# A 90-degree rotation: ScalarE lines each quarter up before VectorE turns it

## The chip, the core and the metric

The kernel runs on one core of one Trainium2 chip. Its time is the device time of one execution in microseconds (us); the figure of a kernel is the median of several runs. Four parts of the core do anything here: SyncE (SP) issues every DMA, the 16 DMA engines move the data, VectorE (DVE) transposes, and ScalarE (ACT) copies. TensorE and GpSimd have no part in the work.

## The reference

```python
batch, c, h, w = 32, 3, 256, 256
x = np.random.randn(batch, c, h, w).astype(np.float32)

def reference(x):
    return np.rot90(x, k=-1, axes=(-2, -1)).astype(np.float32)
```

Each of the 96 images of 256 x 256 fp32 values is turned by 90 degrees clockwise: row h of the input, read from left to right, becomes column 255 - h of the output, read from top to bottom. No arithmetic is done. 25.17 MB are read and 25.17 MB written.

## The kernel before

All images are seen as 24576 rows of 256 values. A slab is 2048 rows (128 partitions times R = 16 rows), and the 12 slabs are taken as six pairs of 4 MB. Each pair has a tile of its own in SBUF, `u0` to `u5`, of 128 partitions x 2 slabs x 4096 values, so no tile is used twice: a pair is loaded into its tile, turned in place, and stored from there.

**Loads.** SP issues twelve loads of 2 MB at the start, one after the other, pair by pair. Pairs 1 to 5 (L59) come in with 16 rows of an image on each partition, in runs of 16 KB; even and odd partitions hold different images. Pair 0 is special (L55): its two slabs come in with two pieces of 8 rows each, second slab first, so that VectorE has a whole slab to begin on when the first 2 MB are there.

**Turning a pair.** VectorE's transpose turns blocks of 32 partitions x 32 values. In `turn_pair` the 32 values of a block are 16 column groups `g`, 16 values (64 bytes) apart, times the two slabs `a`, 4096 values (16 KB) apart; the slab runs fastest. So neighbours in the stream that is read are never neighbours in memory, and the stream that is written (`dst`) hops in the same way, 16 KB and then 64 bytes. A pair is cut in four quarters: the low and high half of the column within a group (`c`), by the low and high half of the row within a partition (`r`). Each quarter is one instruction of 2048 values on each partition. The result of a quarter lands where another quarter's source was:

- (low, low) would land on the source of (high, low), (low, high) on that of (low, low), (high, high) on that of (low, high), and (high, low) on that of (high, high).

The kernel breaks this ring with a spare tile in PSUM: (low, low) is turned into `spare[n % 2]` first (L78), the other three are turned in place, in the order of the ring (L82), and when the last of them is done ScalarE copies the held quarter home in two halves (L84), writing runs of 8 values. There are two spare tiles of 2048 values on each partition, so the next pair's turning does not wait for these copies.

Pair 0 is turned slab by slab (`turn_slab`, L65): one slab into the two spare tiles, the other into the place of the first, and then ScalarE copies the spare tiles into the second slab (L70, two copies of 2048 values).

**Stores.** SP issues two stores of 2 MB for each pair (L97), in the order of the pairs, behind all loads on the same queue. A store waits until its pair is turned and the copies are home.

What sets the order: each engine takes its instructions as they are written in the program; between engines they wait for one another where they touch the same data. SP waits in order, too: a store that is not ready holds back those behind it.

Of the kernel before, what the change touches and what calls it, by code (L numbers as in the profile page):

```python
# [1 line left out]

# [4 lines left out]


@with_exitstack  # L10
def kernel(
    ctx: ExitStack,
    tc: tile.TileContext,
    x: bass.AP,
    out: bass.AP,
):

    nc = tc.nc
    fp32 = mybir.dt.float32

    B, C, H, W = x.shape
    P = nc.NUM_PARTITIONS
    R = 16
    I = 2  # L30
    E = R * W
    n_slabs = B * C * H // (P * R)
    hw = R // 2

    rows_in = x.rearrange("b c h w -> (b c h) w")
    rows_out = out.rearrange("b c h w -> (b c h) w")

    def short(rows):
        return rows.rearrange("(n i p r) w -> n p i (r w)", i=I, p=P, r=R // I)

    def long(rows):
        return rows.rearrange("(n a i m r) w -> n i m a (r w)", a=2, i=I, m=P // I, r=R)

    ld_short, ld_long, st_long = short(rows_in), long(rows_in), long(rows_out)

    pairs = [
        ctx.enter_context(tc.tile_pool(name=f"pair{n}", bufs=1)).tile([P, 2, E], fp32, name=f"u{n}")
        for n in range(n_slabs // 2)
    ]
    psum = ctx.enter_context(tc.tile_pool(name="psum", bufs=1, space=bass.MemoryType.PSUM))  # L50
    spare = [psum.tile([P, E // 2], fp32, name=f"spare{h}") for h in range(2)]


    for s, home in ((1, 0), (0, 1)):
        nc.sync.dma_start(  # L55
            out=pairs[0][:, home].rearrange("p (i f) -> p i f", i=I), in_=ld_short[s])
    for n in range(1, len(pairs)):
        for i in range(I):
            nc.sync.dma_start(out=pairs[n][i::I], in_=ld_long[n, i])  # L59

    def turn_slab(src, dsts):
        s = src.rearrange("p (i r g c) -> p c r g i", i=I, r=R // I, c=R)
        for h, d in enumerate(dsts):
            d = d.rearrange("p (c k r) -> p c r k", c=hw, r=R // I)[:, :, ::-1, ::-1]
            nc.vector.transpose(out=d, in_=s[:, h * hw : (h + 1) * hw])  # L65

    turn_slab(pairs[0][:, 0], spare)
    turn_slab(pairs[0][:, 1], [pairs[0][:, 0, : E // 2], pairs[0][:, 0, E // 2 :]])
    for h in range(2):
        nc.scalar.copy(out=pairs[0][:, 1, h * E // 2 : (h + 1) * E // 2], in_=spare[h])  # L70

    def turn_pair(n):
        u = pairs[n]
        src = u.rearrange("p a (r g c) -> p c r g a", r=R, c=R)
        dst = u.rearrange("p i (c k r) -> p c r k i", c=R, r=R)[:, :, ::-1, ::-1, :]
        held = spare[n % 2]
        low, high = slice(0, hw), slice(hw, R)
        nc.vector.transpose(  # L78
            out=held.rearrange("p (i c k r) -> p c r k i", i=I, c=hw, r=hw)[:, :, ::-1, ::-1, :],
            in_=src[:, low, low])  # L80
        for c, r in ((low, high), (high, high), (high, low)):
            nc.vector.transpose(out=dst[:, c, r], in_=src[:, c, r])  # L82
        for i in range(I):
            nc.scalar.copy(  # L84
                out=u[:, i, : E // 2].rearrange("p (c r) -> p c r", r=R)[:, :, hw:],
                in_=held[:, i * E // 4 : (i + 1) * E // 4].rearrange("p (c r) -> p c r", r=hw))

    for n in range(1, len(pairs)):
        turn_pair(n)
    for n in range(len(pairs)):  # L90
        for a in range(2):
            if n == 0:

                st = rows_out[: 2 * P * R].rearrange("(s i m r) w -> i m s (r w)", s=2, i=I, r=R)[a]
            else:
                st = rows_out.rearrange("(n a i m r) w -> n a m i (r w)", a=2, i=I, m=P // I, r=R)[n, a]
            nc.sync.dma_start(out=st, in_=pairs[n][a::2])  # L97


# [1 line left out]
_INS = ['x']  # L101
_OUTS = [((32, 3, 256, 256), 'float32')]


# [23 lines left out]
```

## Time and profile before

| | |
|---|---|
| Time, median of 3 runs | 123.2 us (122.94 to 123.29) |
| The profiled execution | 122.98 us, of which the profile's span is 121.2 us |
| Busy in the span | VectorE 86.6 us (71%), ScalarE 14.5 us (12%) |
| DMA queue of SP | 50.33 MB, mean 415 GB/s over the span; packets fill 97.9% of 16 engines' span |
| DMA issues | 12 loads and 12 stores of 2048 KB each |

The profile shows one execution. A line such as `L82 DVE STREAM_TRANSPOSE u<-u ... x15 | 54.3, 3619` is a group of instructions: line 82 of the kernel, engine, operation, written and read tile, how many of them, their busy time in us in total, and the mean of one in ns. `SPq` is SP's queue, that is, its waits and DMA issues. "To landing" is the time from a DMA's issue to its last byte. Times in the timeline count from the start of the span.

### The profile page before, as it was taken

The numbers are of one execution on the slowest core, as the hardware profiler recorded it, in microseconds if no ns is written. First come the engines' busy times: TensorE is split into PE (matmuls) and PEld (weight loads), VectorE is DVE, ScalarE is ACT, GpSimd is POOL, SyncE is SP. The second block draws the span as 40 slices with busy tenths as digits, with TensorE's granted clock in tenths as the row PEclk, the third lists the DMA queues.
The fourth block names the chain that finished last, engine by engine and source line by source line (L and its number), as shares of the span: only waits on it lengthen the run. The fifth ranks groups of instructions, "written<-read, shape, count | busy, mean of one in ns | idle before, by whom it ended". The sixth has DMA issues, their size and how long they took to land.

```text
span 121.2 us, 125 instructions
## 1 busy us (share of the span) xinstructions
DVE 86.6 (71%) x24; ACT 14.5 (12%) x13; POOL 0.2 (0%) x4
## 2 busy tenths in 40 slices
DVE  0029999619999999999999999999999970000000
ACT  0000400380000330005000060000600023000000
POOL 0000000000000000000000000000000000000000
DMA  4999999999999999999999999999999999999994
GB/s 87 403 419 433 465 433 433 427 427 433 433 411 422 416 427 433 433 433 433 422 433 433 433 433 433 433 433 433 433 433 433 433 427 427 433 433 433 433 433 184
DMA packets 3713, 50.33 MB, mean 415 GB/s; under 512 B 385, under 2 KB 385, under 8 KB 385
## 3 DMA queue, kind: packets, MB, share of 16 engines
q1 hardware_dynamic: 3712, 50.33, 97.9%
q14 instruction: 1, 0.00, 0.0%
HBM read 25.17 MB, written 25.17 MB: 415 GB/s over the span
## 4 chain that ended last, share of the span: by engine, by line
DVE 60%; issue 13%; DMA 6%; ACT 2%; ACTq 1%
DVE u L82 33%; DVE spare L78 15%; DVE u L65 6%; DMA u<-in_x_dram 6%; DVE spare L65 6%; ACT u L70 2%; ACT u L84 1%; ACTq L123 1%
## 5 line engine op out<-in xcount | busy, mean ns | idle before, releaser
L82 DVE STREAM_TRANSPOSE u<-u 128x2048 f32<-128x2048 f32 x15 | 54.3, 3619 | 0.5
L78 DVE STREAM_TRANSPOSE spare<-u 128x2048 f32<-128x2048 f32 x5 | 17.9, 3574 | 3.7 <-ACT u L70 3.7
L84 ACT COPY u<-spare 128x1024 f32<-128x1024 f32 x10 | 9.6, 1014 | 64.6 <-DVE u L82 64.6
L65 DVE STREAM_TRANSPOSE spare<-u 128x2048 f32<-128x2048 f32 x2 | 7.1, 3585 | 8.3 <-DMA u<-in_x_dram 8.3
L65 DVE STREAM_TRANSPOSE u<-u 128x2048 f32<-128x2048 f32 x2 | 7.8, 3986 | 0.0
L70 ACT COPY u<-spare 128x2048 f32<-128x2048 f32 x2 | 3.6, 1869 | 8.7 <-DVE u L65 8.7
L70 ACT ACT_TABLE_LOAD x1 | 1.3, 1283 | 13.3 <-DMA u<-in_x_dram 13.3
L112 POOL MEMSET const-bfloat16-1.0<- 128x1 bf16 x1 | 0.1, 101 | 0.0
L112 POOL MEMSET const-uint8-127<- 128x1 uint8 x1 | 0.1, 101 | 0.0
L112 POOL MEMSET const-float32-0.0<- 128x1 f32 x1 | 0.1, 98 | 0.2 <-issue 0.2
L112 POOL MEMSET const-float32-1.0<- 128x1 f32 x1 | 0.1, 98 | 0.0
## 6 DMA issues: line engine op xcount, KB each, us to landing
u<-in_x_dram SPq DMA_DIRECT2D x12, 2048.0 KB, 31.1
out_dram<-u SPq DMA_DIRECT2D x12, 2048.0 KB, 28.3
```

The lines of the kernel that those rows point to most:

```text
L65: nc.vector.transpose(out=d, in_=s[:, h * hw : (h + 1) * hw])
L70: nc.scalar.copy(out=pairs[0][:, 1, h * E // 2 : (h + 1) * E // 2], in_=spare[h])
L78: nc.vector.transpose(out=held.rearrange("p (i c k r) -> p c r k i", i=I, c=hw, r=hw)[:, :, ::-1, ::-1, :], in_=src[:, low, low])
L82: nc.vector.transpose(out=dst[:, c, r], in_=src[:, c, r])
L84: nc.scalar.copy(out=u[:, i, : E // 2].rearrange("p (c r) -> p c r", r=R)[:, :, hw:], in_=held[:, i * E // 4 : (i + 1) * E // 4].rearrange ...
L112: nc = _bacc.Bacc("TRN2", target_bir_lowering=False, num_devices=1)
L123: with _tile.TileContext(nc) as tc:
```

## The change

For pairs 1 to 5, VectorE no longer reads the pair's tile. ScalarE copies each quarter (`take`) out of the tile in the order in which VectorE will want it, hopping through memory as VectorE did before, and writes it as one run of 2048 values into a temporary tile (`line_up`). VectorE (`turn`) reads that run and writes the turned quarter straight home, to the same places with the same hops as before. The quarters 0 to 3 are (low, low), (low, high), (high, high), (high, low); quarter 0 goes to `spare[0]`, 1 and 3 to `spare[1]`, and 2 to a new SBUF tile `extra` of 2048 values. The order in the program is take 0, take 1, take 2, turn 1, take 3, turn 2, turn 3, turn 0. The two copies home at the end of each pair are gone.

The load of the first 2 MB is cut in two transfers of 1 MB; both fill the slab that VectorE turns first. Pair 0 is turned as before. The other loads and all stores move the same bytes between the same places in the same order; their code is written anew (`pairs` becomes `groups`, all of size 2).

```diff
+    low, high = slice(0, hw), slice(hw, R)
...
+    sizes = (2,) * 6
+    first = [sum(sizes[:n]) for n in range(len(sizes))]
...
     spare = [psum.tile([P, E // 2], fp32, name=f"spare{h}") for h in range(2)]
+    extra = ctx.enter_context(tc.tile_pool(name="extra", bufs=1)).tile([P, E // 2], fp32, name="extra")
...
-    for s, home in ((1, 0), (0, 1)):
-        nc.sync.dma_start(
-            out=pairs[0][:, home].rearrange("p (i f) -> p i f", i=I), in_=ld_short[s])
-    for n in range(1, len(pairs)):
+    ld = rows_of(rows_in, 0).rearrange("(s i p r) w -> s i p (r w)", s=2, i=2, p=P)
+    home = [groups[0][:, s].rearrange("p (i f) -> p i f", i=2) for s in range(2)]
+    for i in range(2):
+        nc.sync.dma_start(out=home[0][:, i], in_=ld[1, i])
+    nc.sync.dma_start(out=home[1], in_=ld[0].transpose([1, 0, 2]))
+    for n in range(1, len(sizes)):
...
-    def turn_pair(n):
-        u = pairs[n]
+    def turn_group(n):
+        u = groups[n]
         src = u.rearrange("p a (r g c) -> p c r g a", r=R, c=R)
         dst = u.rearrange("p i (c k r) -> p c r k i", c=R, r=R)[:, :, ::-1, ::-1, :]
-        held = spare[n % 2]
-        low, high = slice(0, hw), slice(hw, R)
-        nc.vector.transpose(
-            out=held.rearrange("p (i c k r) -> p c r k i", i=I, c=hw, r=hw)[:, :, ::-1, ::-1, :],
-            in_=src[:, low, low])
-        for c, r in ((low, high), (high, high), (high, low)):
-            nc.vector.transpose(out=dst[:, c, r], in_=src[:, c, r])
-        for i in range(I):
-            nc.scalar.copy(
-                out=u[:, i, : E // 2].rearrange("p (c r) -> p c r", r=R)[:, :, hw:],
-                in_=held[:, i * E // 4 : (i + 1) * E // 4].rearrange("p (c r) -> p c r", r=hw))
+        quarters = ((low, low), (low, high), (high, high), (high, low))
+        temps = (spare[0], spare[1], extra, spare[1])
 
+        def line_up(q):
+            return temps[q].rearrange("p (c r g a) -> p c r g a", c=hw, r=hw, g=R)
+
+        def take(q):
+            c, r = quarters[q]
+            nc.scalar.copy(out=line_up(q), in_=src[:, c, r])
+
+        def turn(q):
+            c, r = quarters[q]
+            nc.vector.transpose(out=dst[:, c, r], in_=line_up(q))
+
+        take(0)
+        take(1)
+        take(2)
+        turn(1)
+        take(3)
+        turn(2)
+        turn(3)
+        turn(0)
```

More of the change, by code (lines that the diff above doesn't have):

```diff
@@ L29 @@
     R = 16
-    I = 2
     E = R * W
-    n_slabs = B * C * H // (P * R)
     hw = R // 2
+    low, high = slice(0, hw), slice(hw, R)
     rows_in = x.rearrange("b c h w -> (b c h) w")
     rows_out = out.rearrange("b c h w -> (b c h) w")
[L38 to L48, printed above, removed]
+    sizes = (2,) * 6
+    first = [sum(sizes[:n]) for n in range(len(sizes))]
+    groups = [
+        ctx.enter_context(tc.tile_pool(name=f"group{n}", bufs=1)).tile([P, s, E], fp32, name=f"u{n}")
+        for n, s in enumerate(sizes)
     ]
@@ L51, with rows_of @@
     spare = [psum.tile([P, E // 2], fp32, name=f"spare{h}") for h in range(2)]
-    for s, home in ((1, 0), (0, 1)):
-        nc.sync.dma_start(
-            out=pairs[0][:, home].rearrange("p (i f) -> p i f", i=I), in_=ld_short[s])
-    for n in range(1, len(pairs)):
+    extra = ctx.enter_context(tc.tile_pool(name="extra", bufs=1)).tile([P, E // 2], fp32, name="extra")
+    def rows_of(rows, n):
+        return rows[first[n] * P * R : (first[n] + sizes[n]) * P * R]
+    ld = rows_of(rows_in, 0).rearrange("(s i p r) w -> s i p (r w)", s=2, i=2, p=P)
@@ L58 @@
+    home = [groups[0][:, s].rearrange("p (i f) -> p i f", i=2) for s in range(2)]
[3 more added lines that the diff above has]
+    for n in range(1, len(sizes)):
+        I = sizes[n]
+        ld = rows_of(rows_in, n).rearrange("(a i m r) w -> i m a (r w)", a=2, i=I, m=P // I)
         for i in range(I):
-            nc.sync.dma_start(out=pairs[n][i::I], in_=ld_long[n, i])
+            nc.sync.dma_start(
+                out=groups[n].rearrange("p s f -> p (s f)").rearrange("p (a f) -> p a f", a=2)[i::I],
+                in_=ld[i])
@@ L61, in turn_slab @@
     def turn_slab(src, dsts):
-        s = src.rearrange("p (i r g c) -> p c r g i", i=I, r=R // I, c=R)
+        s = src.rearrange("p (i r g c) -> p c r g i", i=2, r=R // 2, c=R)
         for h, d in enumerate(dsts):
-            d = d.rearrange("p (c k r) -> p c r k", c=hw, r=R // I)[:, :, ::-1, ::-1]
+            d = d.rearrange("p (c k r) -> p c r k", c=hw, r=R // 2)[:, :, ::-1, ::-1]
             nc.vector.transpose(out=d, in_=s[:, h * hw : (h + 1) * hw])
-    turn_slab(pairs[0][:, 0], spare)
@@ L68 @@
-    turn_slab(pairs[0][:, 1], [pairs[0][:, 0, : E // 2], pairs[0][:, 0, E // 2 :]])
+    u = groups[0]
+    turn_slab(u[:, 0], spare)
+    turn_slab(u[:, 1], [u[:, 0, : E // 2], u[:, 0, E // 2 :]])
     for h in range(2):
-        nc.scalar.copy(out=pairs[0][:, 1, h * E // 2 : (h + 1) * E // 2], in_=spare[h])
-    def turn_pair(n):
-        u = pairs[n]
+        nc.scalar.copy(out=u[:, 1, h * E // 2 : (h + 1) * E // 2], in_=spare[h])
+    def turn_group(n):
+        u = groups[n]
         src = u.rearrange("p a (r g c) -> p c r g a", r=R, c=R)
@@ L88 @@
[L88 to L97, printed above, removed]
+        quarters = ((low, low), (low, high), (high, high), (high, low))
@@ new lines, in turn_group @@
+        turn(3)
+        turn(0)
+    for n in range(1, len(sizes)):
+        turn_group(n)
+    st = rows_of(rows_out, 0).rearrange("(s i m r) w -> i m s (r w)", s=2, i=2, m=P // 2)
+    for a in range(2):
+        nc.sync.dma_start(out=st[a], in_=groups[0][a::2])
+    for n in range(1, len(sizes)):
+        st = rows_of(rows_out, n).rearrange("(a i m r) w -> a m i (r w)", a=2, i=sizes[n], m=P // 2)
+        for i in range(0, sizes[n], 2):
+            for a in range(2):
+                nc.sync.dma_start(out=st[a][:, i : i + 2], in_=groups[n][a::2, i : i + 2])
```

## The prediction

> **What bounds the kernel now.** I read the page's slices and queues first, since 50.33 MB through one core suggest the transfers.
>
> ```profile
> DVE  0029999619999999999999999999999970000000
> ACT  0000400380000330005000060000600023000000
> ...
> DMA  4999999999999999999999999999999999999994
> ...
> q1 hardware_dynamic: 3712, 50.33, 97.9%
> ```
>
> The DMA engines are full from the first slice to the last; VectorE ends a fifth of the span earlier. The windows give the rate of a full stretch:
>
> ```profile
> 55.80:70.20 14.40, 14.30 (x5) 1.93 (x2) 0.00 (x0) 1.00 1.02 432
> 70.20:84.60 14.40, 14.30 (x5) 1.93 (x2) 0.00 (x0) 1.00 1.01 432
> ```
>
> VectorE is busy 14.3 of 14.4 us (one pair), ScalarE 1.93, and the queue moves 432 GB/s. A pair's 4.19 MB of stores take 4.19 / 0.432 = 9.7 us, 4.85 us for each store. So turning a pair (14.4) is slower than storing it (9.7); the transfers bound the end only because a backlog of loads and finished pairs feeds the queue. How much is left of it, the time from a store's issue to its landing says, asked window by window (pairs 2, 3, 4 and 5, two stores each, medians):
>
> ```profile
> out_dram<-u SPq DMA_DIRECT2D x2, 2048.0 KB, 30.6
> ...
> out_dram<-u SPq DMA_DIRECT2D x2, 2048.0 KB, 25.9
> ...
> out_dram<-u SPq DMA_DIRECT2D x2, 2048.0 KB, 21.2
> ...
> out_dram<-u SPq DMA_DIRECT2D x2, 2048.0 KB, 16.5
> ```
>
> The backlog falls by 4.7 us a pair, which is 14.4 - 9.7. Of the last pair, the shortest landing of all stores is 14.4, so with a median of 16.5 the other took 18.6: issued at 101.14 and about 101.8, they land at 115.5 and 120.4, and 0.8 us later the span ends. On an empty queue, 2 MB land sooner, as the first load shows in the chain (0.73 to 8.24):
>
> ```profile
> 0.73 7.51 DMA u<-in_x_dram
> ...
> 26.89 3.62 DVE spare L78
> ...
> 99.19 1.01 ACT u L84
> ```
>
> Hence the slack of the last pair is 14.4 - 7.5 = **6.9 us**: it may be ready at 101.1 + 6.9 = 108.0 instead of 101.1 before anything moves. Later than that, the span ends at ready + 7.5 + 4.85 + 0.8 = ready + 13.2. Time is span plus 122.98 - 121.2 = 1.8; the median of the runs (123.2) is 0.2 above the profiled one, and I add that too: time = ready + 15.2.
>
> The groups of instructions give the prices:
>
> ```profile
> L82 DVE STREAM_TRANSPOSE u<-u 128x2048 f32<-128x2048 f32 x15 | 54.3, 3619 | 0.5
> L78 DVE STREAM_TRANSPOSE spare<-u 128x2048 f32<-128x2048 f32 x5 | 17.9, 3574 | 3.7 <-ACT u L70 3.7
> L84 ACT COPY u<-spare 128x1024 f32<-128x1024 f32 x10 | 9.6, 1014 | 64.6 <-DVE u L82 64.6
> L65 DVE STREAM_TRANSPOSE spare<-u 128x2048 f32<-128x2048 f32 x2 | 7.1, 3585 | 8.3 <-DMA u<-in_x_dram 8.3
> L65 DVE STREAM_TRANSPOSE u<-u 128x2048 f32<-128x2048 f32 x2 | 7.8, 3986 | 0.0
> L70 ACT COPY u<-spare 128x2048 f32<-128x2048 f32 x2 | 3.6, 1869 | 8.7 <-DVE u L65 8.7
> ```
>
> All transposes move 2048 values in 3.57 to 3.99 us, whatever they write to. ScalarE's copies read and write runs: 1869 - 1014 = 855 ns for 1024 more values is 0.835 ns a value.
>
> **The change, part by part.** Call a `take` A and a `turn` D.
>
> *D.* The write stays as in L82, the read becomes a run. Which of the two made the 3.62 us no row says alone: with one and the same read, L65 costs 3585 into `spare` and 3986 into `u`, so the write side does count (0.4 us by its place). Bounds: 1.87 (the nearest row that has runs on both sides, ScalarE's L70) and 3.99 (the dearest transpose). I take 3.62, the row with the same write on the same engine: if either side's hops alone hold the stream at 3.6, curing one cures nothing.
>
> [...]
>
> *A.* Four copies of 2048 values a pair. No row has ScalarE reading with hops. Bounds: not below 1.87 (the same count in runs, L70; hops can't make it cheaper) and up to 3.57 (VectorE reading the very same pattern into the same tile, L78). I take the one between that keeps VectorE's price in engine steps: a hopping value costs VectorE 3574 / 2048 = 1.745 ns; its own step in runs is not shown, so I go by the middle of the two bounds per value (0.835 and 1.745: 1.29) and, since L78 has the same pattern and L70 only the same engine, somewhat above it: 1.4, giving A = 2048 x 1.4 + 0.16 (L84's 1.014 - 1024 x 0.835 ns) = **3.0 us**.
>
> [...]
>
> *The order.* turn 0, the last of a pair, reads `spare[0]`; the next pair's take 0 writes it, so ScalarE waits there until VectorE is done with the whole pair, with take 1 and take 2 queued behind it. VectorE's first turn needs take 1, so it stands idle for takes 0 and 1. Then turn 1 covers take 2. take 3 needs `spare[1]`, which turn 1 frees, and lies beside turn 2; turn 3 and turn 0 follow. With A up to D a pair costs 2A + 4D, with A above D it is 4A + 2D. Handovers between the engines cost 0.02 to 0.05 us each (26.87 to 26.89, 41.46 to 41.49); 0.1 a pair in all.
>
> *Sum.* 2 x 3.0 + 4 x 3.62 + 0.1 = 20.6, less the 0.1 by which two copies in a row overlap (2 x 1.87 took 3.63): **20.5 us a pair** against 14.4. Pair 1 starts at 26.9 as now, after ScalarE's L70. Ready: 26.9 + 5 x 20.5 = 129.4. Time: 129.4 + 15.2 = **144.6 us**.
>
> *Removed.* The copies home: four of five pairs' lie beside VectorE's work (windows: 1.93 of 14.4) and are worth nothing; the last pair's 1.93 us stood before its stores, and the sum has left it out already. VectorE still does four instructions a pair; nothing of its own work goes.
>
> *Loads and stores.* One more issue, 0.43 to 0.46 us of SP by the two of L55. SP's next loads move back by that; hidden, because by 8.3 us it has issued nine loads while only one has landed. Were that cover gone, 0.5 us. VectorE's first turn needs both 1 MB parts, so its start at 8.26 stands. A shorter first issue might start the flow sooner, within the 0.44 us of that issue: -0.4 to +0.5, taken as 0. `extra` and the temporaries have no queue to pass. SP's stores keep their order and now wait for turn 0.
>
> **The rivals.**
>
> *VectorE's reading was the whole cost.* D falls towards 1.87 and the chain stays under the transfers. It decides at a period of (108.0 - 26.9) / 5 = 16.2 us: with A = 1.87, D must be under 3.1; with A = 3.0, 4A + 2D must be under 16.2, so D under 2.1. Then the end is the queue's and the time 123.2, give or take the 0.4 of the first transfer. For it: L82 and L78 read alike, write to different memories, and differ by only 45 ns. Against it: L65's 0.4 us by the write alone. 22 in 100; of these 7 gain over 0.3%, 12 stay within it, 3 lose a little.
>
> *ScalarE becomes the bound.* D falls to 1.87 but A is L78's 3.57: 4 x 3.57 + 2 x 1.87 = 18.0, ready 116.9, time 132. Decides from A above 3.1 at that D. 10 in 100.
>
> *The overlap inside a pair does not come.* If a copy and a turn of one tile wait for each other although they touch different quarters, take 2 stands before turn 1 and take 3 before turn 2: 4A + 4D = 26.5, ready 159.4, time 174.6. The trace of before has no copy beside a turn of the same tile (L84 starts when the last L82 has ended), so it can't exclude this. 6 in 100.
>
> **How the numbers follow.** My forecast (D unchanged, A between its bounds) has 62 in 100. Its own range: A = 1.87 gives 18.25 a pair, ready 118.1, 133.3 us; A = 3.57 gives 21.6, ready 134.9, 150.1 us, with a little above it for D: 133 to 151. The range over the cases must go down to the hidden case: 122.8 to 151. It leaves out the lost overlap (6), gains (7) and an overshoot (about 5). About 0.3%, 0.4 us, is what can be told from no change here: faster 0.07, same 0.12, slower 0.62 + 0.10 + 0.06 + 0.03 = 0.81.
>
> **What would show it.** D: the turns' rows at 3.6 us, three of a pair reading `spare`, one `extra`. A: `take`'s mean near 3.0, bounds 1.87 and 3.57. Order: VectorE idle for two copies, about 6 us, before the first turn of each pair, released by ScalarE, and none between its four turns; ScalarE waiting on VectorE once at each pair's take 0. Transfers: the DMA row, full until about 100 us, shows gaps before the last two pairs' stores, which land in about 7.5 and 12 us instead of 14 and 19. I am wrong if D drops below 3, or the row stays full to the end.

## The result, and the profile after

The changed kernel takes 148.14 us (median of 6 runs, 148.06 to 148.20) against 123.1 us (6 runs): 1.2035 times as long, with a 95% interval of 1.2023 to 1.2047. The profiled execution took 148.19 us, with a span of 146.4 us. The forecast was 144.6 us, slower.

The page's slices and its queue line of the changed kernel:

```profile
DVE  0079993007999108999009998019997039995000
ACT  0003006999920899900999901999802999600000
...
DMA  5999999999999999999999997898000996001995
...
q1 hardware_dynamic: 3728, 50.33, 81.4%
```

The two compute engines now take turns: where one row shows a gap, the other shows nines. The DMA row is full up to about two thirds of the span and then has two empty stretches. The queue has the same 50.33 MB to move, but its packets fill 81.4% of the span and no longer 97.9%. What bounds the kernel is no longer the queue but the chain of copies and transposes.

The groups of instructions, with the time idle before them and who ended it:

```profile
L93 DVE STREAM_TRANSPOSE u<-spare 128x2048 f32<-128x2048 f32 x15 | 53.1, 3587 | 39.6 <-ACT spare L89 39.3
L89 ACT COPY spare<-u 128x2048 f32<-128x2048 f32 x15 | 53.4, 3586 | 28.8 <-DVE u L93 28.3
L89 ACT COPY extra<-u 128x2048 f32<-128x2048 f32 x5 | 18.3, 3652 | 0.0
L93 DVE STREAM_TRANSPOSE u<-extra 128x2048 f32<-128x2048 f32 x5 | 18.1, 3626 | 0.0
```

A turn that reads a run costs 3587 or 3626 ns; before, with hops on both sides (single values far apart in memory, no two of them neighbours), it was 3619. Hardly anything was gained there. A take costs 3586 or 3652 ns. VectorE waits 39.3 us for ScalarE, and ScalarE 28.3 us for VectorE. One pair in the timeline:

```profile
48.19 7.08 ACT L89 COPY spare<-u 128x2048 f32<-128x2048 f32 x2 [7.08 <-DVE u L93]
55.20 3.65 ACT L89 COPY extra<-u 128x2048 f32<-128x2048 f32 x1
55.30 3.61 DVE L93 STREAM_TRANSPOSE u<-spare 128x2048 f32<-128x2048 f32 x1 [7.14 <-ACT spare L89]
58.89 3.63 DVE L93 STREAM_TRANSPOSE u<-extra 128x2048 f32<-128x2048 f32 x1
58.94 3.60 ACT L89 COPY spare<-u 128x2048 f32<-128x2048 f32 x1
62.58 7.01 DVE L93 STREAM_TRANSPOSE u<-spare 128x2048 f32<-128x2048 f32 x2
69.62 3.57 ACT L89 COPY spare<-u 128x2048 f32<-128x2048 f32 x1 [7.08 <-DVE u L93]
```

Takes 0 and 1 stand alone (48.19 to 55.27), then turn 1 lies beside take 2, turn 2 beside take 3, and turns 3 and 0 end at 69.59; the next pair's take 0 starts 0.03 us later. A pair takes 69.62 - 48.19 = 21.43 us, which is 2A + 4D, less 0.1 us by which instructions in a row overlap. The windows show what this does to the queue, one pair early and the last one (busy time of VectorE and ScalarE, then clock, DMA share and GB/s):

```profile
48.18:69.60 21.42, 14.22 (x4) 14.27 (x4) 0.00 (x0) 1.00 1.00 425
...
112.50:133.90 21.40, 14.21 (x4) 14.28 (x4) 0.00 (x0) 1.00 0.46 196
```

Both engines are busy two thirds of the time in each. Early, loads and earlier stores keep the queue at 425 GB/s; at the end it has nothing but the one pair that was finished 21 us before. The last pair is ready at 133.91, its stores are issued at 133.94 and 134.6 and land in 6.8 and 11.0 us, and the span ends at 146.4.

### The profile page after: what moved, and what is told of

The parts are those of the page before. It is cut to its first block, busy times and chain, and to the rows that moved or that the text cites. A ratio compares the mean times of both kernels' runs of the same rounds, so it can differ in the third digit from the quotient of the medians.

```text
span 146.4 us, 137 instructions
## 1 busy us (share of the span) xinstructions
DVE 86.0 (59%) x24; ACT 76.2 (52%) x23; POOL 0.2 (0%) x4
## 2 busy tenths in 40 slices
DMA packets 3728, 50.33 MB, mean 344 GB/s; under 512 B 400, under 2 KB 400, under 8 KB 400
## 3 DMA queue, kind: packets, MB, share of 16 engines
q1 hardware_dynamic: 3728, 50.33, 81.4%
## 4 chain that ended last, share of the span: by engine, by line
ACT 38%; DVE 35%; issue 11%; DMA 5%; DVEq 2%; SPq 0%
ACT spare L89 36%; DVE u L93 25%; DVE u L69 5%; DVE spare L69 5%; DMA u<-in_x_dram 5%; DVEq L141 2%; ACT u L75 1%; SPq L55 0%; DVEq L69 0%
## 5 line engine op out<-in xcount | busy, mean ns | idle before, releaser
L93 DVE STREAM_TRANSPOSE u<-spare 128x2048 f32<-128x2048 f32 x15 | 53.1, 3587 | 39.6 <-ACT spare L89 39.3
L89 ACT COPY spare<-u 128x2048 f32<-128x2048 f32 x15 | 53.4, 3586 | 28.8 <-DVE u L93 28.3
L89 ACT COPY extra<-u 128x2048 f32<-128x2048 f32 x5 | 18.3, 3652 | 0.0
L93 DVE STREAM_TRANSPOSE u<-extra 128x2048 f32<-128x2048 f32 x5 | 18.1, 3626 | 0.0
L69 DVE STREAM_TRANSPOSE spare<-u 128x2048 f32<-128x2048 f32 x2 | 7.1, 3586 | 8.3 <-DMA u<-in_x_dram 8.3
L75 ACT ACT_TABLE_LOAD x1 | 1.3, 1283 | 13.2 <-DMA u<-in_x_dram 13.2
L69 DVE STREAM_TRANSPOSE u<-u 128x2048 f32<-128x2048 f32 x2 | 7.8, 3982 | 0.0
```

What stands on the lines that cost most here:

```text
L75: nc.scalar.copy(out=u[:, 1, h * E // 2 : (h + 1) * E // 2], in_=spare[h])
L89: nc.scalar.copy(out=line_up(q), in_=src[:, c, r])
L93: nc.vector.transpose(out=dst[:, c, r], in_=line_up(q))
```

## The experiments

The theory: the take's hops cost as much as the turn's did; curing one side of the turn cures nothing; and the tile `spare[0]`, which the next pair's take 0 must wait for, puts two takes of each pair on the path. The rivals: the engines slow each other down when they work side by side; the transpose itself costs 3.6 us; the cut load matters.

**One part alone: the cut load (e1).** In the kernel before:

```diff
-    for s, home in ((1, 0), (0, 1)):
-        nc.sync.dma_start(out=pairs[0][:, home]..., in_=ld_short[s])
+    for i in range(I):
+        nc.sync.dma_start(out=pairs[0][:, 0]...[:, i], in_=ld_short[1][:, i])
+    nc.sync.dma_start(out=pairs[0][:, 1]..., in_=ld_short[0])
```

> The kernel before, with only the first 2 MB load cut in two loads of 1 MB (the smallest part of the change, done alone). The prediction: VectorE needs both parts, so its first transpose still starts at 8.26 us and the queue is full to the end; time unchanged at 123.1 us within 0.3%. The rival, that a smaller first transfer brings the data sooner: the DMA row starts up to 0.4 us earlier and the time falls by as much.

Measured: 123.35 us against 123.02, ratio 1.0026 (1.0015 to 1.0037). VectorE starts at 8.24, as expected, and the time is within the expected 0.3%, but clear of the noise it is 0.33 us longer. The rival's gain did not come, and where the queue is the bound the cut costs a third of a microsecond, out of 25. In the changed kernel it holds nothing up at the start: pair 1's first take starts at 26.73 us, where pair 1's first turn started at 26.89 before.

**Without the wait at the pair's border (e2).** In the changed kernel:

```diff
+    ring = [spare[0], spare[1], extra]
...
-        temps = (spare[0], spare[1], extra, spare[1])
+        x, y, z = ring
+        temps = (x, y, z, y)
+        ring[:] = [z, y, x]
```

> The changed kernel, except that the three temporary tiles change roles from pair to pair: take 0 goes into the tile that turn 2 of the pair before has freed, take 1 into that of turn 3, take 2 into that of turn 0. The same 40 instructions with the same operands' shapes. If the lost time is the wait of take 0 for turn 0 (theory): takes 0 and 1 of a pair slip beside turns 3 and 0 of the one before, a pair takes 4 x 3.6 + 0.2 = 14.7 us instead of 21.4, the last pair is ready at about 107.5, and the time is back at 123.1 to 123.6. If instead ScalarE and VectorE slow each other down when they work side by side all the time (rival): A and D rise above 3.7, a pair stays well over 16 us and the time over 128.

Measured: 123.42 us against 123.02, ratio 1.0035 (1.0016 to 1.0054). One pair's window and the main groups:

```profile
62.80:77.40 14.60, 14.24 (x4) 14.46 (x6) 0.00 (x0) 1.00 1.01 431
```

```profile
L93 ACT COPY spare<-u 128x2048 f32<-128x2048 f32 x15 | 53.4, 3585 | 1.1 <-DVE u L97 0.6
L97 DVE STREAM_TRANSPOSE u<-spare 128x2048 f32<-128x2048 f32 x15 | 53.3, 3597 | 12.1 <-ACT spare L93 11.6
```

A pair takes 14.6 us, both engines are busy nearly all of it, and neither instruction is dearer than in the changed kernel, beyond 10 ns (3585 and 3597 against 3586 and 3587). The rival of mutual slowing falls, and all but 0.4 us of the loss is gone with the wait: 10.7 of VectorE's remaining 11.6 us of waiting come ahead of the first turn of pair 1.

**The same with one first load (e6).** Edit: in e2, `nc.sync.dma_start(out=home[0], in_=ld[1].transpose([1, 0, 2]))` in place of the two loads of 1 MB.

> The kernel with the rotated temporaries, with the first 2 MB in one load again, so that only ScalarE's and VectorE's work differs from the kernel before. Theory (all that was left of the change there was the cut load's 0.3 us): within 0.1% of before, 123.0 to 123.1. Rival (ScalarE's and VectorE's work in the tiles slows the transfers): 0.2% to 0.4% above before.

Measured: 123.08 us against 123.07, ratio 1.0001 (0.9993 to 1.0010). The path through ScalarE, with forty instructions of 3.6 us where the kernel before has twenty and ten copies of 1 us, then costs nothing that can be measured, since it stays under the transfers. What e2 had left over was the cut load.

**What makes a turn cost 3.6 us (e3).** The kernel before, with the in-place transposes of each pair changed:

```diff
-        for c, r in ((low, high), (high, high), (high, low)):
-            nc.vector.transpose(out=dst[:, c, r], in_=src[:, c, r])
+            if n == 1: nc.vector.transpose(out=dst[:, c, r], in_=here)
+            if n == 2: nc.vector.transpose(out=there, in_=src[:, c, r])
+            if n == 3: nc.vector.transpose(out=there, in_=here)
+            if n == 4: nc.vector.transpose(out=there, in_=pairs_here)
+            if n == 5: nc.vector.transpose(out=pairs_there, in_=here)
```

(`here` and `there` are runs of 2048 values in the pair's tile; the other two go through runs of two values.)

> The kernel before, with the three in-place transposes of each pair reading and writing other places (the order of the values in the output is left out): pair 1 reads a run and writes with hops as before, pair 2 reads with hops and writes a run, pair 3 reads and writes runs, pair 4 reads runs of two values and writes runs, pair 5 reads runs and writes runs of two. Theory (either side's hops alone hold the stream): pairs 1 and 2 stay at 3.5 to 3.6 us an instruction, pair 3 falls to about 2.2, and pairs 4 and 5 are near pair 3. Rival 1 (the transpose itself costs 3.6 whatever the pattern): all five at 3.5 to 3.6. Rival 2 (reads and writes add): pairs 1 and 2 clearly under 3.6, with pair 3 lowest.

The groups; lines 89 to 97 are pairs 1 to 5:

```profile
L89 DVE STREAM_TRANSPOSE u<-u 128x2048 f32<-128x2048 f32 x3 | 10.9, 3635 | 0.1
L91 DVE STREAM_TRANSPOSE u<-u 128x2048 f32<-128x2048 f32 x3 | 10.8, 3609 | 0.1
...
L97 DVE STREAM_TRANSPOSE u<-u 128x2048 f32<-128x2048 f32 x3 | 6.9, 2312 | 0.1
L95 DVE STREAM_TRANSPOSE u<-u 128x2048 f32<-128x2048 f32 x3 | 6.9, 2312 | 0.1
L93 DVE STREAM_TRANSPOSE u<-u 128x2048 f32<-128x2048 f32 x3 | 6.9, 2311 | 0.1
```

Hops on the write alone: 3635 ns. On the read alone: 3609. On both (L82 before): 3619. On neither: 2311, and runs of two are as good as one long run (2312). So for these hops the two sides don't add, and either is enough. Both rivals fall. One row stays outside this: pair 0's L65 into `u` reads with hops and writes SBUF in steps of 32 bytes, and took 3986 ns, where the same read into PSUM took 3585. Whether those steps alone cost that much, or both sides together, was not run. This kernel also shows the other side of the slack: its last pair is turned and copied at 89.3 us instead of 101.1, and its time is 123.11 us in its one run: a faster VectorE is worth nothing here.

**What makes a take cost 3.6 us (e4).** The changed kernel, with other places for the takes:

```diff
-            nc.scalar.copy(out=line_up(q), in_=src[:, c, r])
+            if n == 1: nc.scalar.copy(out=run, in_=v[:, q * Q : (q + 1) * Q])
+            if n == 2: nc.scalar.copy(out=run, in_=two[...])
+            if n == 3: nc.scalar.copy(out=run, in_=v.rearrange("p (x t) -> p t x", t=4)[:, q])
+            if n == 4: nc.scalar.copy(out=run.rearrange("p (g t) -> p t g", t=16), in_=v[:, q * Q : (q + 1) * Q])
+            if n == 5: nc.scalar.copy(out=line_up(q), in_=src[:, c, r])
```

> The changed kernel, with ScalarE's takes reading and writing other places (the order of the values in the output is left out): pair 1 reads and writes runs; pair 2 reads runs of two values; pair 3 reads single values 16 bytes apart; pair 4 reads a run and writes single values 64 bytes apart; pair 5 is as in the change. If the hops alone made A 3.58 (theory): pair 1 takes 1.87 us an instruction, pair 2 near it, pairs 3 and 4 well above, 3 us or more. If the working tile or the work beside VectorE made it (rival): pair 1 stays near 3.6. The sum by 2A + 4D: pair 1 takes 2 x 1.87 + 4 x 3.62 = 18.2 us from its first take to its last turn, pair 5 21.5.

The groups; lines 95, 97, 99, 101 and 104 are pairs 1 to 5:

```profile
L99 ACT COPY spare<-u 128x2048 f32<-128x2048 f32 x3 | 11.2, 3743 | 14.2 <-DVE u L108 14.2
L104 ACT COPY spare<-u 128x2048 f32<-128x2048 f32 x3 | 11.0, 3663 | 5.0 <-DVE u L108 4.9
...
L97 ACT COPY spare<-u 128x2048 f32<-128x2048 f32 x3 | 5.9, 1973 | 10.3 <-DVE u L108 10.3
L95 ACT COPY spare<-u 128x2048 f32<-128x2048 f32 x3 | 5.5, 1880 | 3.7 <-DVE u L108 3.7
L101 ACT COPY spare<-u 128x2048 f32<-128x2048 f32 x3 | 5.5, 1867 | 14.2 <-DVE u L108 14.2
...
L101 ACT COPY extra<-u 128x2048 f32<-128x2048 f32 x1 | 3.6, 3618 | 0.0
```

Runs: 1880 ns; runs of two: 1973; single values, 16 bytes apart already: 3743. ScalarE pays for hops as VectorE does; pair 1, copied out of the same tiles, falls to the price of runs, its take 3 beside a turn too, so the rival falls. The theory has one miss: writing with hops into PSUM (L101 into `spare`) costs 1867, no more than a run, while the same hops into the SBUF tile `extra` cost 3618. The second half of the expectation, 18.2 us for pair 1, did not come (19.5 us, from 26.64 to 46.17) and was not a test: the takes read other quarters' places here, and VectorE's first turn of that pair started only at 32.18 us, when take 2 had ended too (32.15; take 1 had ended at 30.3).

**The hops moved to the PSUM side (e5).** That miss allows a smaller A with the values still where they belong; neighbours in the stream land 1 KB apart in PSUM. In the changed kernel, for takes 0, 1 and 3:

```diff
-            nc.scalar.copy(out=line_up(q), in_=src[:, c, r])
...
+                runs = u.rearrange("p a (x c) -> p a x c", c=R)
+                runs = runs.rearrange("p a (r g) c -> p a r g c", r=R)[:, :, r, :, c]
+                nc.scalar.copy(
+                    out=temps[q].rearrange("p (c r g a) -> p a r g c", c=hw, r=hw, g=R), in_=runs)
```

> The changed kernel, with takes 0, 1 and 3 reading runs of 8 values from the tile and writing single values with hops into the PSUM tile, so that the same values lie at the same places as before; take 2, into the SBUF tile, is as in the change. Theory (A is what its hopping side in SBUF costs, and a pair takes 2A + 4D): takes 0, 1 and 3 fall from 3.58 to 1.87 us, as pair 4 of the run of take patterns did; turns stay at 3.6; a pair falls from 21.4 to 2 x 1.87 + 4 x 3.6 = 18.2, the last pair is ready at 26.7 + 91 = 117.7 and the time is 117.7 + 12.5 + 1.8 = 132.0. Rival (a take is bound by the number of values that it hops over, on either side): takes stay near 3.6 and the time at 148.1.

Measured: 129.8 us against 123.07, ratio 1.0543 (1.0529 to 1.0557). The groups and one pair's window:

```profile
L99 DVE STREAM_TRANSPOSE u<-spare 128x2048 f32<-128x2048 f32 x15 | 53.2, 3592 | 22.2 <-ACT spare L94 22.2
L94 ACT COPY spare<-u 128x2048 f32<-128x2048 f32 x15 | 27.7, 1871 | 34.8 <-DVE u L99 34.8
```

```profile
44.40:62.10 17.70, 14.00 (x4) 9.10 (x4) 0.00 (x0) 1.00 1.00 417
```

The takes into PSUM fall to 1871 ns, and a pair from 21.43 to 17.75 us (44.40 to 62.15), by twice the 1.71 us that a take lost and 0.26 that the turns lost. So it is the two takes ahead of the first turn that count, not all four. Expected were 18.2 a pair and 132.0 us; the difference is 4 x 3.6 for turns that take 14.0 together, because one starts about 0.1 us before the profile has the last one ended.

**Hops in PSUM (e8).** Each pair's work in the kernel before replaced by three instructions between its tile and PSUM (`hops` steps 64 bytes through `held`):

```diff
+            if n == 1: nc.vector.transpose(out=hops, in_=run)
+            if n == 2: nc.vector.transpose(out=run, in_=hops)
+            if n == 3: nc.scalar.copy(out=run, in_=hops)
+            if n == 4: nc.vector.transpose(out=held, in_=run)
+            if n == 5: nc.vector.transpose(out=run, in_=held)
```

> The kernel before, with each of pairs 1 to 5 replaced by three instructions between its tile and a PSUM tile (what they move is not the rotation): pair 1, VectorE reads a run and writes PSUM with hops of 64 bytes; pair 2, VectorE reads PSUM with such hops and writes a run; pair 3, ScalarE does that; pair 4, VectorE reads a run and writes a run in PSUM; pair 5, VectorE reads a run in PSUM and writes a run. If hops cost nothing in PSUM (theory, from ScalarE's 1867 ns): VectorE at 2.3 us in all four, ScalarE at 1.87. If that holds for ScalarE's writes alone: pairs 1 and 2 at 3.5 or more, pair 3 at 3 or more.

The groups; lines 83 to 91 are pairs 1 to 5:

```profile
L89 DVE STREAM_TRANSPOSE spare<-u 128x2048 f32<-128x2048 f32 x3 | 7.0, 2327 | 12.1 <-DMA u<-in_x_dram 12.0
L83 DVE STREAM_TRANSPOSE spare<-u 128x2048 f32<-128x2048 f32 x3 | 7.0, 2326 | 3.8 <-ACT u L70 3.7
L91 DVE STREAM_TRANSPOSE u<-spare 128x2048 f32<-128x2048 f32 x3 | 6.7, 2289 | 2.7 <-DMA u<-in_x_dram 2.7
L85 DVE STREAM_TRANSPOSE u<-spare 128x2048 f32<-128x2048 f32 x3 | 6.7, 2274 | 0.0
L87 ACT COPY u<-spare 128x2048 f32<-128x2048 f32 x3 | 5.4, 1874 | 15.8 <-DMA u<-in_x_dram 15.8
```

With hops in PSUM, VectorE takes 2326 (write) and 2274 (read), without them 2327 and 2289; ScalarE reads them at 1874. In PSUM these hops are free for both engines, reading and writing (ScalarE's write is the 1867 of e4). This fits L78 and L65 into `spare`: their 3.58 us are then the price of the read in SBUF alone, as e3's 3609 for the read alone says too, though their own steps in PSUM were not run by themselves.

**Two loads cut (e7).** Edit: in the kernel before, both loads of pair 0 in two of 1 MB.

> The kernel before, with both loads of pair 0 cut in two of 1 MB. If each DMA more costs the queue a fixed 0.3 us: 0.6 us above before, ratio 1.005. If the 0.3 us came from one odd transfer leaving the 16 engines out of step: about 0.3 us or less, ratio 1.000 to 1.003.

Measured: 123.52 us against 123.07, ratio 1.0034 (1.0022 to 1.0046). A fixed 0.3 us for each DMA more (ratio 1.005) lies outside the interval; about 0.2 us each would fit this interval and that of one cut (1.0026), so a smaller fixed cost stays possible. The DMA rows of 110 to 122 us, of before, of e1 and of e7, show one difference:

```profile
DMA  9393939392939393939393939595959600000000
```

```profile
DMA  5969797989798989999999999897989630000000
```

```profile
DMA  7979898989999897979797979696959090000000
```

Before, the row goes 9 and 3 in turn to the end; with a cut load the row is more even and ends a slice (0.3 us) later. That the 16 engines run out of step there, as the expectation had it, is a guess that no run shows. The row of e6, with one load, looks as before; that of e2, with a cut load, is back at 9 and 3 before its end and still ends later. So the cut load and the 0.3 us go together in these runs, and what makes the 0.3 us stays open.

## Why the prediction was right

- **The bound and the slack.** Right. The queue was the bound, with some 7 us to spare by the landing times. Of these e2 shows 5.1: its last pair is ready at 106.2 us instead of 101.1, and its time is 0.4 us above that of before; e6, the same work with one first load, takes 123.08 us, as before. In the changed kernel, once the last pair was ready at 133.9, the span followed it by 12.5 us (forecast 13.2: on the empty queue the first of the last stores landed in 6.8 us, where I had taken 7.5 from the first load).
- **D unchanged.** Right, 3.59 and 3.63 for a taken 3.62, and for the reason given: e3 has either side's hops at 3.6 alone (3635 ns on the write, 3609 on the read), and L82, which hops on both, lies between the two (3619 ns, 1.77 a value). L65 into `u`, with its other steps, took 3986 ns (1.95 a value).
- **A.** The term that was mis-sized: 3.0 taken, 3.58 measured, at the upper bound (3.57). I had split the difference between ScalarE's price for runs and VectorE's for these very hops. The row with the same pattern was the nearer one: L78 3574 ns, the takes into `spare` 3575 in the median and 3586 in the mean. The hops make that price on either engine: VectorE's read of the same places took 3609 ns, and 2311 in runs (e3); ScalarE's copy in runs took 1880 (e4). Two takes a pair on the path, 0.58 too low each, make 5 x 1.16 = 5.8 us.
- **The order.** Right: 2A + 4D, VectorE idle for 7.1 us ahead of each of pairs 2 to 5, ScalarE once at take 0. e2 and e6 show that this wait is the whole loss.
- **The sum.** 5.8 us too little for A, 1.1 too much for the turns and handovers (14.35 a pair, not 14.58), 0.7 too much for the tail, and 0.4 for the start (26.73, not 26.9) and for the median's 0.2: 144.6 + 5.8 - 2.2 = 148.2. That the smaller errors all went against A's was luck: without them the forecast would have been 5.8 us low instead of 3.5. (The lower end of the range takes 18.25 us a pair where its own terms give 18.2, which is 0.1 us in the time.)
- **The cut load.** Taken as 0, with -0.4 to +0.5 as bounds. It is +0.3 where the queue is the bound (e1). In the changed kernel the queue isn't, and what it costs there was not measured by itself.
- **The rivals.** D did not fall, so the hidden case and ScalarE as the bound are out. Copies and turns of one tile do run side by side (55.20 and 55.30 above), so the lost overlap is out.

## What to carry to other kernels

With the hops of this change, an instruction that hops on both sides in SBUF costs no more than one that hops on one side (3619 ns against 3609 and 3635), so splitting it into a copy that hops in and a transpose that hops out pays the same price twice (3586 and 3587) and saves nothing. For other steps this has to be measured: L65 into `u` took 3986. If such a staging is wanted, let the staging tile be in PSUM and put the copy's hops on that side, where they were free (e5: 1871 ns, with single values read in SBUF 3586). That alone did not save this change: the turn still hops on its write, the wait at the pair's border stays, and e5 was slower than the kernel before (129.8 us). And before judging a stage by its instructions, look at who frees its buffers: here the same 40 instructions cost 25 us or nothing (148.14 us in the changed kernel, 123.08 in e6), depending on whether the next pair's first copy went into the tile that was freed last or into the one freed first.

## What the runs showed of the hardware

- ScalarE and VectorE pay the same to read the single values of this change with hops in SBUF (takes 3575 in the median, L78 3574 ns, for 2048), though in runs they differ (1.87 and 2.31 us). Other steps have other prices: 3743 ns for ScalarE's reads 16 bytes apart, 3986 for VectorE's L65 with writes 32 bytes apart. Runs of two values bring both near the price of long runs (1.97 and 2.31 us).
- In PSUM, steps of 64 bytes cost neither engine anything, reading or writing (ScalarE 1867 to 1874 ns, in runs 1869 and 1880; VectorE 2274 and 2326, in runs 2289 and 2327), nor ScalarE's writes 1 KB apart (e5: 1871).
- Both engines side by side, each hopping in SBUF, in the same pair's tile or in two pairs' tiles, keep their prices (e2: 3585 and 3597), and the queue keeps 431 GB/s beside them.
